# Moving the next sequence's norms into the MLP passes, and the last attention group's rotated rows ahead of weight loads

## The chip, the cores and the metric

The kernel runs on all 8 cores of one Trainium2 chip, as the same program on different data: each core computes two sequences of the batch of 16. The metric is the device time of the slowest core, in microseconds (us). Cores 0 to 3 are one die of the chip and cores 4 to 7 the other. In some executions of before the cores of one die show a lower granted clock of TensorE than the other die's and take longer: in one run of before 0.930 to 0.940 and 2206.7 to 2223.7 us on cores 4 to 7, against 0.973 to 0.977 and 2133.2 to 2148.7 us on cores 0 to 3. Such runs are called slow and are not compared with fast ones.

## The reference

One layer of an encoder, then a final norm. Only the order of the parts matters here. Sequences have 2048 positions of 1024 channels, the memory has 256 positions, the MLP is 4096 wide.

```python
def reference(x, mem, norm_mix, w_in, ..., norm_final):
    h = rms_norm(x, norm_mix[l])                       # "norm 1"
    x = x + hybrid_mixer(h, ...)     # projections; DFT branch; 3 attention groups with
                                     # rotary on the first 16 of 64 head dims; gates; merge
    h = rms_norm(x, norm_cross[l])
    mem_n = rms_norm(mem, norm_mem[l])                 # "memory norm"
    x = x + memory_cross_attention(h, mem_n, ...)
    h = rms_norm(x, norm_mlp[l])
    x = x + sq_relu_mlp(h, w_up[l], w_down[l])
    return rms_norm(x, norm_final)                     # "final norm"
```

## The kernel before

A helper records every operation with its reads and writes and then sets the semaphores; so every instruction has the helper's line (L148) in the profile, and all of SBUF is one tile called `arena`. A sequence is worked in four tiles (`tg`) of 512 positions. "A unit" below is eight matmuls into one PSUM bank (PSUM is the memory that TensorE's matmuls write to, `ps` in the views) and what evicts it. In the views PE is TensorE, PEld its weight loads, DVE VectorE, ACT ScalarE, POOL GpSimd and SP SyncE.

**The norm.** Squares are made by ScalarE, added up over eight channel chunks by GpSimd (`eng='pool'`), split into a high and a low bf16 half, summed over partitions by two matmuls with a matrix of ones, and turned into a reciprocal root by ScalarE. VectorE then scales.

```python
def norm_sq(k, src, n=512, ns=0, eng='pool', lag=False):
    ...
    def add(i):
        if i > 0:
            tt(eng, acc_, acc_, sq[i % 2][:, 0:n], ALU.add)
    act(sq[k % 2][:, 0:n] if k else acc_, src, AF.Square)
    ...
    add(k)
    if k == 7:
        act(hi, acc_, AF.Copy)
        tt('dve', lo, acc_, hi, ALU.subtract)

def norm_rstd(n=512, ns=0, r=None):
    ...
    mm(o, ones, hi[:, 0:n], True, False)
    mm(o, ones, lo[:, 0:n], False, True)
    act(r, o, AF.Ln, scale=1.0 / D, bias=eps)
    act(r, r, AF.Exp, scale=-0.5)

pend = []                       # generators with work put off
def popp(fc, first=3, steps=2): # after unit fc: take `steps` steps of it, from unit `first` on
    ...
```

**The last MLP pass and the sequence boundary.** The MLP goes in four passes over a quarter of its width each; `xT` is the residual and stays in SBUF. In the last pass (3) the kernel also makes the final norm, and norm 1 of the next sequence's tiles 0 to 2.

```python
def up(p_, tg, nxt=None):
    for fc in range(8):
        ...                                       # 8 matmuls
        act(r_, psf(b), AF.Relu)
        tt('dve', a2T[tg % 2][:, fc, :], r_, r_, ALU.mult)
        if nxt is not None:
            norm1_sq(b_ + 1, nxt, [fc], ns=1)     # next sequence's squares
        popp(fc, 3, 4 if p_ == 3 and not last_seq else 2)

def down(p_, tg, t0=0, n=512):
    for fc in range(8):
        ...                                       # 8 matmuls
        tt('dve', x_, o, x_, ALU.add)
        if p_ == 3:
            norm_sq(fc, x_, n, ...)               # final norm's squares
        popp(fc, 3, 4 if p_ == 3 and not last_seq else 2)
...
up(3, 0)
up(3, 1, nxt(0))
down(3, 0)
pend.append(fin_out(0))                           # final norm: 8 scales, store
if not last_seq:
    pend.append(fin_next(0))                      # next sequence's norm 1: 8 scales
...                                               # the same for the tiles that follow
```

The next sequence begins with its projections. Its tile 3 and its memory are still not normed at that point:

```python
for tg in range(NTG):
    for i in range(6):
        ...                                       # projection units
    if tg == 0:
        flush()
        load_dft()                                # loads mem and the DFT matrix
        norm1_sq(b_, 3, ns=1)
    elif tg == 1:
        norm1_fin(b_, 3, ns=1)
        mem_sq()
    elif tg == 2:
        mem_fin()
```

**The rotated rows.** Of each head only 16 of 64 rows are rotated. They are gathered by small DMAs, rotated by VectorE, and put back by eight DMAs of 64 KB (`rb`). The attention of the group can't start before. For group 2 two weight loads of 1 MB each (`bload(3)`, `bload(4)`) were issued at about the same time.

```python
def rotate(g):
    ...
    for c in range(2):
        pairs = ...
        OP('sp', 'dma_group', pairs, reads=[rot], writes=[q_[:, c, :], k_[:, c, :]], dma_key='rb%d' % c)

def proj_gen(g):
    ...
    for i in range(8):
        if 2 <= i < 6:
            next(rg, None)                        # rotate, put back
        if i == 5:
            if g == 1:
                load_rope(2)
            else:
                bload(4)
        v_unit(g, 2 * i, FB)
        yield

interleave(attn(0), proj_gen(1), ...)
interleave(attn(1), proj_gen(2), ...)
bload(3)
...
interleave(attn(2), gate_first(), lambda k: k % 2)
```

**The start.** ScalarE casts the small Fourier weights in `load_consts` (`cp('act', fmb, fm32)`), and both halves of tile 0 are normed before the first projection unit.

The softmax here doesn't subtract the row's maximum and nothing guards it: scores larger than these inputs give would overflow.

## Time and profile before

| | before |
|---|---|
| time, median of 6 runs | 2147.29 us (2146.23 to 2207.45) |
| profiled execution, slowest core (5) | 2147.3 us |
| TensorE busy | 1992.4 us (93%) |
| TensorE idle | 147.4 us |
| mean granted TensorE clock, core 5 | 0.974 |

The page's first lines, the TensorE rows of its 40 slices, and the first line of the chain of waits. In the slices each digit is tenths: of TensorE's busy time in the row PE, of the granted clock in the row PEclk. One slice is 53.7 us.

```profile
span 2147.3 us, 30868 instructions; the slowest of 8 cores (2133.0 to 2147.3 us)
...
PE 1992.4 (93%) x10282; PEld 975.2 (45%) x10282; DVE 989.5 (46%) x1553; ACT 771.6 (36%) x1310; POOL 420.8 (20%) x391
...
PE   3789879999999999999878996999999999999996
...
PEclk9899999999999999999999998999999999999998
...
PE 82%; DVE 6%; ACT 4%; issue 3%; DMA 2%; POOL 2%; SPq 0%; ACTq 0%; DVEq 0%; POOLq 0%
```

TensorE bounds the kernel: 82% of the chain of waits is TensorE itself. What is left to gain is where the slices are below 9: the start (slices 1 to 3), slices 5 and 6 (the last attention groups of the first sequence), slices 20 to 22 (the boundary between the sequences), slice 25 (the last attention group of the second), and the end.

The windows view compares a pure MLP stretch with the boundary (core 5; the columns are the stretch, its length, then busy time with the number of instructions for PE, PEld, DVE, ACT and POOL, then granted clock, DMA share and GB/s).

```profile
660.00:1036.00 376.00, 376.00 (x1744) 170.48 (x1742) 133.81 (x229) 80.99 (x138) 34.49 (x34) 1.00 0.21 42
1036.00:1149.00 113.00, 88.19 (x365) 36.79 (x363) 77.72 (x101) 46.05 (x82) 56.80 (x49) 0.90 0.50 153
```

The MLP stretch has no idle TensorE and full clock, 0.2156 us a matmul (376 over 1744). At that pace the 365 matmuls of the boundary are worth 79 us; it took 113, with 24.8 us idle and a clock of 0.90. What TensorE waited for there (the waits view of core 5, us in total, times, longest):

```profile
PE ps L148 <- ACT arena L148: 21.8, 5, 4.9
PE ps L148 <- DVE arena L148: 3.0, 7, 0.7
```

Five waits for ScalarE, at the matmuls of five norms. From the order of the program and the number of matmuls between them they are the final norms of tiles 1 and 2 in the last pass, then, among the next sequence's projections, the final norm of tile 3, norm 1 of tile 3 and the memory norm. The timeline of core 0 shows them one by one (start, us, what ran, and in brackets the idle time before it and what ended it):

```profile
1044.80 0.59 PE L148 MATMUL ps<-arena 128*128 128x512 bf16 x1 [4.97 <-ACT arena L148]
...
1081.89 0.59 PE L148 MATMUL ps<-arena 128*128 128x512 bf16 x1 [4.97 <-ACT arena L148]
...
1107.31 0.38 PE L148 MATMUL ps<-arena 128*128 128x512 bf16 x1 [4.34 <-ACT arena L148]
...
1124.51 0.44 PE L148 MATMUL ps<-arena 128*128 128x512 bf16 x1 [4.22 <-ACT arena L148]
...
1139.14 0.27 PE L148 MATMUL ps<-arena 128*128 128x256 bf16 x1 [1.75 <-ACT arena L148]
```

The first two gaps lie in the last MLP pass, the other three in the next sequence's projections. A gap can cost more than itself: in it or at its end the granted clock mostly falls to 0.5 for 3.4 or 6.8 us (10.2 us before attention 2 on core 5). On core 5 the gap that ends at 1050.4 us goes with half clock from 1048.4 to 1055.2 us. At half clock matmuls start every 0.43 us (1051.3 to 1055.1 us), then every 0.2156 again.

Why ScalarE is late is seen on VectorE. Scale instructions of 128x512 f32 take 0.74 us alone (0.68 us each in a row) and twice that beside GpSimd's adds. The timeline of VectorE, core 5:

```profile
1055.79 4.54 DVE L148 SCALAR_TENSOR_TENSOR arena<-arena 128x512 f32<-128x512 f32 x3 [0.50 <-ACT arena L148]
...
1060.59 2.73 DVE L148 SCALAR_TENSOR_TENSOR arena<-arena 128x512 f32<-128x512 f32 x4
```

Three took 1.51 us each while GpSimd was adding squares (1.28 us an add), and the next four 0.68 us each when it was not. The trace shows the doubling, not what the two engines contend for. VectorE's next work is then late, ScalarE's squares of it are late (on core 5 ScalarE waited 33.3 us for VectorE between 1036 and 1149 us), and TensorE waits for the norm. The last of the five waits has one more cause: the load of the memory took 8.5 us from issue to landing, and ScalarE waited 5.9 us for it.

The rows of group 2, in the DMA view of core 5 between 247 and 256 us (out and in, queue, count, KB each, median us from issue to landing), and TensorE's timeline there:

```profile
arena<-wb POOLq DMA_DIRECT2D x2, 1024.0 KB, 11.7
arena<-arena SPq DMA_DIRECT2D x8, 64.0 KB, 9.4
```

```profile
261.50 2.00 PE L148 MATMUL ps<-arena 64*128 64x128 bf16 x11 [9.02 <-DMA arena<-arena]
```

Eight rows of 64 KB take 9.4 us beside two loads of 1 MB, and TensorE waits 9.02 us for them. Those of group 1, with no weight load issued beside them (193 to 198 us), take 2.3 us. So the rows of group 2 are slowed although they are on another queue than the loads.

### The profile page before, as it was taken

How to read it: one execution, taken by the hardware profiler on the slowest of the kernel's cores; microseconds unless marked ns; L12 is line 12 of the kernel's file. 1: busy time of each engine (PE TensorE's matmuls, PEld its weight loads, DVE VectorE, ACT ScalarE, POOL GpSimd, SP SyncE). 2: the span in 40 equal slices, each digit the busy share in tenths (PEclk: the TensorE clock that was granted, in tenths of full speed). 3: DMA queues.
4: the chain of work that ended last, by engine and by line, in shares of the span. 5: the costliest groups of instructions: out<-in, count | busy, mean ns of one | idle time of the engine just before them, and what ended most of it. 6: DMA issues, size and time to landing. Idle time of an engine off the chain costs nothing.

```text
span 2147.3 us, 30868 instructions; the slowest of 8 cores (2133.0 to 2147.3 us)
## 1 busy us (share of the span) xinstructions
PE 1992.4 (93%) x10282; PEld 975.2 (45%) x10282; DVE 989.5 (46%) x1553; ACT 771.6 (36%) x1310; POOL 420.8 (20%) x391
## 2 busy tenths in 40 slices
PE   3789879999999999999878996999999999999996
PEld 2445534455444444444334553444544444444443
DVE  4555572355453323233776456434545533333345
ACT  4445452246442120214434554423554311111143
POOL 2200013352330000004451000334413100000033
PEclk9899999999999999999999998999999999999998
DMA  8532406067020303121354422424540022121213
GB/s 211 115 75 59 79 19 178 1 118 128 11 79 1 68 11 59 20 50 30 130 150 117 85 60 50 157 40 79 93 85 1 1 40 40 30 50 20 40 40 118
DMA packets 32076, 147.04 MB, mean 68 GB/s; under 512 B 4529, under 2 KB 10802, under 8 KB 21682
## 3 DMA queue, kind: packets, MB, share of 16 engines
q0 software_dynamic: 11808, 75.50, 19.8%
q1 hardware_dynamic: 19680, 69.22, 9.8%
q8 instruction: 87, 1.43, 0.3%
q14 instruction: 67, 0.55, 0.1%
q10 hardware_dynamic: 434, 0.35, 0.1%
HBM read 197.48 MB, written 16.78 MB: 100 GB/s over the span
## 4 chain that ended last, share of the span: by engine, by line
PE 82%; DVE 6%; ACT 4%; issue 3%; DMA 2%; POOL 2%; SPq 0%; ACTq 0%; DVEq 0%; POOLq 0%
PE ps L148 82%; DVE arena L148 6%; ACT arena L148 3%; POOL arena L148 2%; DMA arena<-arena 1%; DMA arena<-mem 1%; DMA arena<-fmix 0%; SPq L146 0%; ACT L148 0%; DVEq L142 0%; ACTq L142 0%; POOLq L142 0%; ACTq L148 0%; SPq L148 0%; SPq L142 0%
## 5 line engine op out<-in xcount | busy, mean ns | idle before, releaser
L148 PE MATMUL ps<-arena 128*128 128x512 bf16 (+4 forms) x10282 | 1992.4, 357 | 147.4 <-ACT arena L148 92.8
L148 PEld LDWEIGHTS ps<-arena 128*128 128x128 bf16 (+1 forms) x10282 | 975.2, 100 | 1164.4 <-issue 247.4
L148 ACT ACTIVATE arena<-ps 128x512 bf16<-128x512 f32 (+4 forms) x812 | 488.9, 624 | 1001.3 <-PE ps L148 851.1
L148 DVE TENSOR_TENSOR arena<-arena 128x512 bf16<-128x512 bf16 (+7 forms) x607 | 315.0, 539 | 647.4 <-ACT arena L148 632.3
L148 POOL TENSOR_TENSOR arena<-arena 128x512 f32<-128x512 f32 (+2 forms) x299 | 366.6, 1227 | 746.2 <-ACT arena L148 461.5
L148 DVE TENSOR_TENSOR arena<-ps,arena 128x512 f32<-128x512 f32 (+3 forms) x376 | 293.3, 791 | 251.5 <-PE ps L148 250.4
L148 ACT ACTIVATE arena<-arena 128x512 f32<-128x512 f32 (+5 forms) x452 | 260.6, 589 | 340.9 <-DVE arena L148 203.0
L148 DVE SCALAR_TENSOR_TENSOR arena<-arena 128x512 bf16<-128x512 f32 (+3 forms) x296 | 218.4, 786 | 56.1 <-ACT arena L148 55.6
L148 POOL DMA_DIRECT2D arena<-wb x62 | 33.6, 543 | 778.8 <-PE ps L148 715.6
L148 DVE SCALAR_TENSOR_TENSOR arena<-arena,ps 128x512 f32<-128x512 f32 x128 | 81.9, 683 | 151.4 <-PE ps L148 146.8
L148 DVE SCALAR_TENSOR_TENSOR arena<-ps,arena 128x512 f32<-128x512 f32 x64 | 43.5, 687 | 32.8 <-PE ps L148 32.8
L148 ACT ACTIVATE arena<-ps,arena 128x512 f32<-128x512 f32 (+1 forms) x37 | 23.6, 638 | 21.1 <-DVE arena L148 16.2
L148 POOL DMA_DIRECT2D arena<-wa x20 | 10.9, 554 | 102.7 <-PE ps L148 101.6
L148 POOL MEMSET arena<- 128x2048 bf16 x6 | 10.9, 1812 | 89.3 <-PE ps L148 89.3
L148 DVE COPY arena<-ps 128x1024 f32<-128x1024 f32 (+3 forms) x20 | 20.2, 1009 | 6.3 <-PE ps L148 6.3
L148 DVE CAST arena<-ps 128x512 bf16<-128x512 f32 (+1 forms) x36 | 20.0, 580 | 4.4 <-PE ps L148 3.5
L148 DVE STREAM_SHUFFLE arena<-arena 128x2048 bf16<-128x2048 bf16 x6 | 13.7, 2287 | 0.0
L148 ACT ACT_TABLE_LOAD x9 | 11.5, 1283 | 5.9 <-PE ps L148 4.6
L148 DVE LOAD_MASK_SELECT arena<-arena x6 | 0.1, 14 | 3.4 <-DMA arena<-arena 3.4
L148 DVE CAST arena<-arena 128x1 bf16<-128x1 f32 x8 | 1.2, 153 | 0.4
L148 DVE MEMSET arena<- 128x1 bf16 (+2 forms) x6 | 0.8, 130 | 1.2 <-PEq L211 1.1
L211 POOL MEMSET const-float32-0.0<- 128x1 f32 x1 | 0.1, 99 | 0.5 <-issue 0.5
(3 smaller groups left out, 0.3 us busy)
## 6 DMA issues: line engine op xcount, KB each, us to landing
arena<-wb POOLq DMA_DIRECT2D x62, 1024.0 KB, 9.2
arena<-x SPq DMA_DIRECT2D x8, 2048.0 KB, 12.6
out<-arena SPq DMA_DIRECT2D x28, 512.0 KB, 2.7
arena<-x SPq DMA_DIRECT2D x24, 512.0 KB, 8.7
arena<-wa POOLq DMA_DIRECT2D x20, 512.0 KB, 9.3
arena<-rope SPq DMA_DIRECT2D x6, 1024.0 KB, 9.2
arena<-arena SPq DMA_DIRECT2D x96, 64.0 KB, 4.2
arena<-x SPq DMA_DIRECT2D x16, 256.0 KB, 10.8
```

What stands on the lines that cost most here:

```text
L148: ins = getattr(eo, o['name'])(*o['args'], **o['kw'])
L211: nc = bass.Bass("TRN2", target_bir_lowering=False)
```

## The change

The intent is to take three things off TensorE's way. Core of the diff, with cuts marked:

1. **Boundary.** The next sequence's x is loaded twice: in pass 1 its squares are made, in pass 2 the memory norm, and in pass 3 only the scales are left (from a second load of x in half tiles). The next sequence's projections then have no norm of their own to make; what is left there is the final norm of tile 3 and the last scales. The final norm's matmuls are taken from the second unit after it is queued (`popp(fc, 1)`) instead of the fourth, in both sequences. In the first sequence `popp` also takes two steps of put-off work a unit instead of four.

```diff
-    def up(p_, tg, nxt=None):
+    def up(p_, tg, hook=None):
...
-            if nxt is not None:
-                norm1_sq(b_ + 1, nxt, [fc], ns=1)
-            popp(fc, 3, 4 if p_ == 3 and not last_seq else 2)
+            if hook is not None:
+                hook(fc)
+            popp(fc, 1 if p_ == 3 else 3)
...                                        (popp in down() likewise)
+    rs = [view(Y0 + i * 2048, 512, F32) for i in range(NTG)]   # kept reciprocal roots
+    def fin_st(tg):
+        norm_rstd(512, 1, rs[tg])
+        yield
+    def sq_st(tg, fc):
+        norm_sq(fc, xst[:, fc, :], ns=1)
...
+    def fin_next(tg, b_=b_):               # pass 3: scales alone, 256 wide
+        for i in (2 * tg, 2 * tg + 1):
+            for c in range(8):
+                stt(hT[...], xh[i % 3][:, c, :], gains[:, 0, c:c + 1], rs[tg][...], ALU.mult, ALU.mult)
+                yield
+            if i + 3 < 8:
+                load_xh(i + 3)
...
+    def hook(tg):
+        if last_seq or p_ == 0:
+            return None
+        if p_ == 1:
+            return lambda fc: sq_st(tg, fc)
+        return (lambda fc: norm_sq(fc, memst2[:, fc, :], 256)) if tg == 1 else None
...
     # next sequence's projections
-    if tg == 0:
-        flush()
-        load_dft()
-        norm1_sq(b_, 3, ns=1)
-    elif tg == 1:
-        norm1_fin(b_, 3, ns=1)
-        mem_sq()
-    elif tg == 2:
-        mem_fin()
+        popp(i, 0, 2 if tg else 0)
+    load_dft()
```

2. **Rows.** Weight loads 3 and 4 are issued later and wait for group 2's rows; the last load of the rotary table is issued earlier in the projections.

```diff
-            bload(4)                       # in proj_gen(2), unit 5
-    bload(3)                               # after attention 1
+    if (n, k) == (0, 1):                   # in gate_first, beside attention 2
+        bload(3, back.values())            # back: the DMAs that put the rows back
+        bload(4, back.values())
```

3. **Start.** VectorE casts the Fourier weights where they are used, and the second half of tile 0 is finished after two projection units.

```diff
-    cp('act', fmb, fm32)
+    cp('dve', fmb, fm32)                   # in make_wz, later
...
-    for h in range(2):
-        norm1_sq(0, 0, ns=h, t0=h * 256, n=256, eng=0)
-        norm1_fin(0, 0, h, h * 256, 256)
-        wk = aload(1 + h)
+    norm1_sq(0, 0, ns=0, t0=0, n=256, eng=0)
+    norm1_fin(0, 0, 0, 0, 256)
+    aload(1)
+    norm1_sq(0, 0, ns=1, t0=256, n=256, eng=0)
+    wk = aload(2)
...
-    (0, 0, 256, {3: [lambda: sq1(0)]}),
+    (0, 0, 256, {1: [lambda: norm1_fin(0, 0, 1, 256, 256)], 3: [lambda: sq1(0)]}),
```

More of the change, by code (lines that the diff above doesn't have):

```diff
@@ L398, in bslot, with bload @@
             return view(R0 + BSLOT[n] * 8192, 4096)
-        def bload(n):
-            wdma(bslot(n), dr['wb'][n])
+        def bload(n, after=()):
+            wdma(bslot(n), dr['wb'][n], after)
         ASLOT = [2, 3, 0, 1, 6, 7, 4, 5, 6, 7]
@@ L412, in build_program @@
         xin = [view(o, 4096, F32, pat="p (c t) -> p c t", c=8) for o in (M0 + 16384, Y0, X0 + 16 * KB, X0 + 32 * KB)]
-        def xb(b_, tg):
-            return tg if b_ == 0 else tg % 2
         def load_xin(b_, tg, t0=0, n=512, after=()):
             src = dr['x'][b_, tg].rearrange("p (c t) -> p c t", c=8)
-            i = xb(b_, tg)
+            i = tg
             return [dma('sp', xin[i][:, 2 * h:2 * h + 2, t0:t0 + n], src[:, 2 * h:2 * h + 2, t0:t0 + n],
@@ L424, in norm1_sq @@
             for k in ks:
-                norm_sq(k, xin[xb(b_, tg)][:, k, t0:t0 + n], n, ns, eng)
+                norm_sq(k, xin[tg][:, k, t0:t0 + n], n, ns, eng)
         def norm1_fin(b_, tg, ns=0, t0=0, n=512):
             norm_rstd(n, ns)
-            norm_apply(0, [xin[xb(b_, tg)][:, c, t0:t0 + n] for c in range(8)],
+            norm_apply(0, [xin[tg][:, c, t0:t0 + n] for c in range(8)],
                        [hT[:, c, tg * 512 + t0:tg * 512 + t0 + n] for c in range(8)], n)
@@ L516, in gather @@
                 OP('sp', 'dma_group', rows, reads=[qkv_views(g)[which]], writes=[rot], dma_key='rg%d' % which)
+            back = {}
             def rotate(g):
@@ L528, in rotate @@
                     q_, k_, _ = qkv_views(g)
-                    OP('sp', 'dma_group', pairs, reads=[rot], writes=[q_[:, c, :], k_[:, c, :]], dma_key='rb%d' % c)
+                    back[c] = OP('sp', 'dma_group', pairs, reads=[rot], writes=[q_[:, c, :], k_[:, c, :]], dma_key='rb%d' % c)
             def v_unit(g, n0, banks):
@@ L609, in load_dft @@
             def load_dft():
-                dma('sp', memst, dr['mem'][b_].rearrange("p (c m) -> p c m", c=8), 'mem')
+                if b_ == 0:
+                    dma('sp', memst, dr['mem'][b_].rearrange("p (c m) -> p c m", c=8), 'mem')
                 dma('sp', dftm, dr['dft'].rearrange("p (k n t) -> p k n t", k=4, n=4), 'dft')
@@ L802, in proj_gen @@
                     qk_unit(g, which, c, tg, FB, 'act')
+                    if n == 1 and g == 2:
+                        load_rope(2)
                     if n == 7:
@@ L816, in proj_gen @@
                         next(rg, None)
-                    if i == 5:
-                        if g == 1:
-                            load_rope(2)
-                        else:
-                            bload(4)
                     v_unit(g, 2 * i, FB)
@@ L1050, in down @@
                         norm_sq(fc, x_, n, 0 if n == 512 else t0 // 256)
-                    popp(fc, 3, 4 if p_ == 3 and not last_seq else 2)
+                    popp(fc, 1 if p_ == 3 else 3)
             rstd2 = view(Y0 + 8192, 512, F32)
@@ L1067, in fin_out, with load_st @@
                     yield
-            for p_ in range(3):
-                up(p_, 0)
+            xst = view(M0 + 16384, 4096, F32, pat="p (c t) -> p c t", c=8)
+            xh = [view(o, 2048, F32, pat="p (c t) -> p c t", c=8) for o in (M0 + 16384, M0 + 24576, Y0 + 8192)]
+            rs = [view(Y0 + i * 2048, 512, F32) for i in range(NTG)]
+            def load_st(tg):
+                for h in range(4):
+                    dma('sp', xst[:, 2 * h:2 * h + 2, :], dr['x'][b_ + 1, tg].rearrange("p (c t) -> p c t", c=8)[:, 2 * h:2 * h + 2, :], 'st%d' % h)
@@ new lines, in fin_st, with load_xh @@
+            def fin_st(tg):
[3 more added lines that the diff above has]
+                norm_sq(fc, xst[:, fc, :], ns=1)
+                if fc == 7 and tg + 1 < NTG:
+                    load_st(tg + 1)
+            def load_xh(i):
+                tg, t0 = i // 2, i % 2 * 256
+                for h in range(2):
+                    dma('sp', xh[i % 3][:, 4 * h:4 * h + 4, :],
+                        dr['x'][b_ + 1, tg].rearrange("p (c t) -> p c t", c=8)[:, 4 * h:4 * h + 4, t0:t0 + 256], 'xh%d%d' % (i % 3, h))
@@ new lines, in fin_next, with mem_next @@
+            def fin_next(tg, b_=b_):
+                for i in (2 * tg, 2 * tg + 1):
+                    t0 = i % 2 * 256
+                    for c in range(8):
+                        stt(hT[:, c, tg * 512 + t0:tg * 512 + t0 + 256], xh[i % 3][:, c, :], gains[:, 0, c:c + 1],
+                            rs[tg][:, t0:t0 + 256], ALU.mult, ALU.mult)
+                        yield
+                    if i + 3 < 8:
+                        load_xh(i + 3)
+            def mem_next():
+                norm_rstd(256)
+                yield
+                for c in range(8):
+                    stt(memn[:, c, :], memst2[:, c, :], gains[:, 2, c:c + 1], rstd[:, 0:256], ALU.mult, ALU.mult)
+                    yield
@@ new lines, in build_program @@
+            memst2 = view(Y0 + 8192, 2048, F32, pat="p (c m) -> p c m", c=8)
+            for p_ in range(3):
+                def hook(tg):
[4 more added lines that the diff above has]
+                    return (lambda fc: norm_sq(fc, memst2[:, fc, :], 256)) if tg == 1 else None
+                if p_ == 1 and not last_seq:
+                    load_st(0)
+                    dma('sp', memst2, dr['mem'][b_ + 1].rearrange("p (c m) -> p c m", c=8), 'mem')
+                up(p_, 0, hook(0))
@@ L1071, in build_program @@
                 for tg in range(NTG):
+                    if p_ == 1 and not last_seq:
+                        pend.append(fin_st(tg))
+                    if p_ == 2 and tg == 1 and not last_seq:
+                        pend.append(mem_next())
                     if tg + 1 < NTG:
-                        up(p_, tg + 1)
+                        up(p_, tg + 1, hook(tg + 1))
                     if tg == NTG - 2:
@@ L1080, in build_program @@
                     bload(23 + 4 * p_)
-            nx = None if last_seq else b_ + 1
-            def fin_next(tg, b_=b_):
-                norm_rstd(ns=1)
-                yield
-                for c in range(8):
-                    stt(hT[:, c, tg * 512:(tg + 1) * 512], xin[tg % 2][:, c, :], gains[:, 0, c:c + 1], rstd, ALU.mult, ALU.mult)
-                    yield
-                if tg < 2:
-                    load_xin(b_ + 1, tg + 2)
-            def nxt(tg):
-                return None if last_seq else tg
             if not last_seq:
-                load_xin(b_ + 1, 0)
-                load_xin(b_ + 1, 1)
+                for i in range(3):
+                    load_xh(i)
                 aload(0)
                 aload(1)
-            up(3, 0)
-            up(3, 1, nxt(0))
-            down(3, 0)
-            pend.append(fin_out(0))
-            if not last_seq:
-                pend.append(fin_next(0))
-            up(3, 2, nxt(1))
-            down(3, 1)
-            pend.append(fin_out(1))
-            if not last_seq:
-                pend.append(fin_next(1))
-            up(3, 3, nxt(2))
-            if not last_seq:
-                aload(2)
-                aload(3)
-            down(3, 2)
-            pend.append(fin_out(2))
-            if not last_seq:
-                pend.append(fin_next(2))
+            for tg in range(NTG):
+                up(3, tg)
+                if not last_seq:
+                    pend.append(fin_next(tg))
+                    if tg == 3:
+                        aload(2)
+                        aload(3)
+                if tg:
+                    down(3, tg - 1)
+                    pend.append(fin_out(tg - 1))
             if last_seq:
```

## The prediction

> **What bounds it now.** The page: TensorE is busy 1992 of 2147 us, and the chain of waits is 82% TensorE. By windows, the pure matmul stages (320-625, 650-1036, 1365-1670, 1683-2110 us) have no idle TensorE. Loss sits at four places: the start (45.9 us idle up to 105 us), each sequence's last attention group (gaps of 9.0 us at 252.5 and 7.9 us at 1296.7), the sequence boundary 1036-1149 us (24.4 us idle), and the tail. Each gap is also followed by 3.4-10 us of 0.5 granted clock. [...]
>
> **The boundary.** Its 363 matmuls are worth 78 us at the undisturbed stages' pace; it takes 113 us. In the last MLP pass GpSimd adds squares for two norms (1.27 us each, two sets of seven per 27.5 us) while VectorE's scale instructions, 0.7-0.75 us alone, take about 1.54 us beside it [...]. VectorE lags a whole down-pass, then norms' matmuls wait 3.4-5 us, five times, the last three inside the next sequence (tile 3's norms, memory's). The change moves squares to pass 1 (ACT has room: 0.6+0.63 of 1.72 us a unit), memory norm to pass 2, and leaves pass 3 only scales (64 of 0.41 us for 32 of 0.7) with half of GpSimd's adds. It loads x again (8.4 MB, DMA nearly idle). [...] Gain 32 us.
>
> **Rotated rows.** Alone they land in 2.28 us (attention group 1); in group 2, among two weight loads, in 7-10 us. With the loads behind them the last needed row lands about 1 us after TensorE runs out: saves 8.0 and 7.0 us of idle, plus 2 us each of half clock: 19 us.
>
> **Start.** ACT waits 11.1 us for the small Fourier weights; x itself is complete at 14.5 us, so this gives about 1.4 us. Units ahead of the second half's norm give 2 us. Gain 3.5 us.
>
> **Loss.** In the last pass the final norm's matmuls are now placed after two units instead of four. Their operands come 4.6 us after the down-pass ends, two units are 3.4 us: about 1.15 us twice, and 1 us at the tail. Cost 3.3 us.
>
> Sum: 2147 - 32 - 19 - 3.5 + 3.3 = 2096, plus 2 for what I miss.
>
> **Predicted: 2098 us, 2086 to 2113.** Chances: faster by over 2% 0.72, within 2% 0.27, slower 0.01.
>
> **Right if:** between the last MLP passes of sequence 0 and its successor's V projection TensorE is busy at full clock with under 4 us idle; MLP pass 1 shows GpSimd and ACT busier and TensorE still full; rows of group 2 land in about 2.3 us, the gaps before attention 2 shrink to 1 us, weight loads follow them.
>
> **Wrong if:** VectorE and GpSimd saturate in pass 3 (gaps of several us at the final norm persist); scales wait for the second x load and block VectorE; the Fourier matrix load collides with sequence 1's first rotated rows; attention 2 turns out bound by ACT and VectorE.

2147 - 32 - 19 - 3.5 + 3.3 is 2095.8, put as 2096, and 2098 with the 2 us for what I missed. A term of the boundary's 32 us is an estimate that 2 to 3 us of waits would remain in pass 3; without it the boundary is the 35 us between 113 and 78. Two phrases go further than the trace of before, core 5: not each gap is followed by half clock (those of 19.3 and 8.9 us at the very start are not), and the DMA engines that were to load x again were 0.21 busy between 660 and 1036 us.

## The result and the profile after

| | before | after |
|---|---|---|
| time, median (lowest to highest; runs) | 2146.46 us (2143.63 to 2207.45; 20) | 2097.47 us (2094.72 to 2099.19; 10) |
| ratio of fast runs, with 95% interval | 1 | 0.9765 (0.9748 to 0.9782) |
| TensorE idle, core 5 | 147.4 us | 101.8 us |
| mean clock, core 5 | 0.974 | 0.983 |
| read from HBM | 197.48 MB | 205.87 MB |

Ratios here and below are the mean time of one kernel's fast runs over the mean of the other's of the same rounds, so they are not quite the ratio of the medians quoted beside them.

```profile
span 2115.7 us, 30871 instructions; the slowest of 8 cores (2089.6 to 2115.7 us)
...
PE 2007.4 (95%) x10282; PEld 980.3 (46%) x10282; DVE 982.1 (46%) x1586; ACT 771.5 (36%) x1309; POOL 418.8 (20%) x391
...
PE   4889979999999999999999988999999999999996
...
PEclk9989999999999999999999999999999999999887
...
PE 84%; DVE 5%; ACT 4%; issue 3%; DMA 2%; POOL 2%; SPq 1%; ACTq 0%; DVEq 0%; POOLq 0%
```

The page is of core 2, at 2115.7 us, while the median is 2097. The cores view says why:

```profile
core 2: 2115.7 us, clock 0.970
...
core 5: 2089.6 us, clock 0.983
...
die 1 (median of its cores): 2092.6 us, clock 0.983
```

In this execution the cores of die 0 had long stretches at a clock of 0.81: cores 2 and 3 for 159 us from 1933.8 and 1933.6 us of their spans (the last slices of PEclk show it for core 2), cores 0 and 1 most of the time from 35 to 195 us of theirs. What set it off the traces do not show. The eleven other runs of the same kernel do not show it (clocks of 0.981 to 0.985 on every core), so everything below is read from die 1, most of it from core 5.

The stages that answer to those shown of before, core 5:

```profile
660.00:1012.00 352.00, 352.00 (x1634) 159.68 (x1633) 138.35 (x255) 95.43 (x170) 56.67 (x55) 1.00 0.34 78
1012.00:1093.00 81.00, 81.00 (x377) 36.71 (x376) 60.93 (x102) 28.80 (x48) 32.70 (x28) 1.00 0.51 135
```

The boundary now runs as the MLP does: no idle, full clock, 0.2149 us a matmul. In the waits view TensorE has no wait at all between 986 and 1110 us, where before it had twelve. In the earlier window GpSimd and ScalarE took on work (56.7 us against 34.5, and 95.4 against 81.0) and TensorE did not notice. In the last pass the scales are narrower and less stretched (0.57 us where 0.48 is the time with no add beside them; in before, core 0, the two full-width forms took 0.87 and 0.96 us where 0.74 is the time alone), and GpSimd has 28 adds where before it had 45 (core 0, 975 to 1090 us). The groups of VectorE and GpSimd by form, core 5, 960 to 1080 us (busy, mean ns of one, idle before):

```profile
L148 DVE SCALAR_TENSOR_TENSOR arena<-arena 128x256 bf16<-128x256 f32 x64 | 33.7, 566 | 0.0
...
L148 POOL TENSOR_TENSOR arena<-arena 128x512 f32<-128x512 f32 x28 | 36.9, 1318 | 70.7 <-ACT arena L148 70.6 <-POOL arena L148 0.2
```

The rows of group 2, in the same two views (DMA from 242 to 252 us):

```profile
arena<-wb POOLq DMA_DIRECT2D x2, 1024.0 KB, 10.7
arena<-arena SPq DMA_DIRECT2D x8, 64.0 KB, 2.3
```

```profile
247.62 5.19 PE L148 MATMUL ps<-arena 64*128 64x128 bf16 x48 [0.98 <-DMA arena<-arena]
```

They land in 2.3 us, and the wait is 0.98 us.

Where the time came from, as the mean over the four cores of die 1 in the two profiled executions. The stages are cut at places that both traces have:

| stage | before, us | after, us | gain |
|---|---|---|---|
| start to the last matmul before attention 2 | 251.6 | 248.1 | 3.6 |
| from there to the wait before the branch units (rows) | 49.7 | 42.4 | 7.4 |
| from there to the first norm of sequence 0's mixer | 333.2 | 334.3 | -1.1 |
| from there to attention 0 of sequence 1 (boundary) | 537.6 | 502.5 | 35.1 |
| to attention 2 of sequence 1 | 120.6 | 120.9 | -0.3 |
| rows, sequence 1 | 52.8 | 47.3 | 5.5 |
| the mixer of sequence 1 | 329.2 | 328.6 | 0.6 |
| the rest, with the last MLP pass and the tail | 465.5 | 468.6 | -3.1 |
| sum | 2140.2 | 2092.6 | 47.5 |

The entries are rounded one by one. The first line should not be trusted to a microsecond: the moment at which a core reaches attention 2 differs by up to 11 us between the cores of one execution.

### The profile page after: what moved, and what is told of

It reads as the page before. It is cut to its first block, busy times and chain, and to the rows that moved or that the text cites. A ratio compares the mean times of both kernels' runs of the same rounds, so it can differ in the third digit from the quotient of the medians.

```text
span 2115.7 us, 30871 instructions; the slowest of 8 cores (2089.6 to 2115.7 us)
## 1 busy us (share of the span) xinstructions
PE 2007.4 (95%) x10282; PEld 980.3 (46%) x10282; DVE 982.1 (46%) x1586; ACT 771.5 (36%) x1309; POOL 418.8 (20%) x391
## 3 DMA queue, kind: packets, MB, share of 16 engines
HBM read 205.87 MB, written 16.78 MB: 105 GB/s over the span
## 4 chain that ended last, share of the span: by engine, by line
PE 84%; DVE 5%; ACT 4%; issue 3%; DMA 2%; POOL 2%; SPq 1%; ACTq 0%; DVEq 0%; POOLq 0%
PE ps L148 84%; DVE arena L148 5%; ACT arena L148 4%; POOL arena L148 2%; DMA arena<-arena 1%; DMA arena<-x 1%; SPq L146 0%; DMA arena<-wa 0%; ACT L148 0%; ACTq L142 0%; DVEq L142 0%; SPq L148 0%; POOLq L142 0%; SPq L142 0%
## 5 line engine op out<-in xcount | busy, mean ns | idle before, releaser
L148 DVE TENSOR_TENSOR arena<-arena 128x512 bf16<-128x512 bf16 (+8 forms) x607 | 310.8, 531 | 610.3 <-ACT arena L148 595.0
L148 ACT ACTIVATE arena<-arena 128x512 f32<-128x512 f32 (+3 forms) x451 | 261.4, 590 | 330.4 <-DVE arena L148 200.8
```

What stands on the lines that cost most here:

```text
L148: ins = getattr(eo, o['name'])(*o['args'], **o['kw'])
```

## The experiments

Edits are against the kernel named. "Us" are medians.

### The three parts alone

**rows_only**: before, with part 2 of the diff and nothing else.

> The kernel before with the row part alone: the two weight loads wait for the rotated rows, and the last rotation table is loaded earlier. My theory (the rows are slow only because two weight loads are in flight with them): rows of the last group land in about 2.3 us, the TensorE gaps ahead of attention 2 shrink from 5-9 us (5 on even cores, 9 on odd) to about 1 us, total 16 us faster than before (2130, range 2126 to 2135). Rival (attention 2 is bound by ACT and VectorE, earlier rows only move the wait into it): the gap shrinks but the total moves by under 5 us.

Measured: 2132.66 us, ratio 0.9926 (0.9914 to 0.9938), 16 us less. The waits before attention 2 were 0.98 to 1.05 us on every core of the trace, where before they were 5 to 6 or 9. As expected.

**start_only**: before, with part 3 and nothing else.

> The kernel before with the start part alone: the cast of the small Fourier matrix moved off ACT's queue, and the second half tile's norm placed after two projection units. My theory: 3 to 5 us faster (2142), seen as an earlier first square on ACT and an earlier end of the first projections. Rival (the first 50 us are bound by the arrival of x, DMA engines 75-91% busy there): under 1.5 us.

Measured: 2146.54 us, ratio 0.9993 (0.9979 to 1.0006): 1.5 us less by the means, and the interval includes nothing at all. The change did what it said at the start. ScalarE's wait for the Fourier weights is gone from the timeline of core 5, first before, then in this run:

```profile
13.89 2.92 ACT L148 ACTIVATE arena<-arena 128x128 bf16<-128x128 f32 x9 [11.12 <-DMA arena<-fmix]
```

```profile
5.47 0.72 ACT L148 ACTIVATE arena<-arena 128x256 f32<-128x256 f32 x2 [2.69 <-DMA arena<-x]
```

TensorE reached the DFT stage at 113.9 us instead of 116.6, as the mean of eight cores. Then attention 0 waits for the rotated rows of group 0, which travel beside weight loads 0 and 1. Core 4, before and in this run:

```profile
135.86 7.50 PE L148 MATMUL ps<-arena 64*128 64x192 bf16 x30 [5.86 <-DMA arena<-arena]
```

```profile
135.13 1.62 PE L148 MATMUL ps<-arena 64*128 64x192 bf16 x6 [7.95 <-DMA arena<-arena]
```

TensorE arrived earlier and waited longer: as the mean of eight cores attention 0 began at 135.0 us instead of 136.5. At attention 2 the mean lead was 0.8 us. A miss, with the gain turned into a wait. It is not the rival's case either: had the arrival of x held the start up, there would be no lead at the DFT stage.

**boundary_only**: before, with part 1, but with the last sequence's final norm left where it was.

```diff
-    popp(fc, 1 if p_ == 3 else 3)
+    popp(fc, 1 if p_ == 3 and not last_seq else 3)
```

> The kernel before with the boundary part alone (next sequence's squares in MLP pass 1, memory norm in pass 2, scales from a second load of x in pass 3), with the last sequence's final norms left where they were. My theory: the five gaps of 3-5 us between 1036 and 1149 us and their half-clock stretches go, total 34 us faster (2112, range 2107 to 2117). Rival (new waits in pass 3, for VectorE or the second x load, give a good part back): gaps of several us stay in pass 3 and the gain is under 28 us.

Measured: three of six runs were slow, so the median (2171.47) says nothing. The fast ones took 2113.83, 2114.39 and 2117.05 us, ratio 0.9846 (0.9831 to 0.9861), 33 us less. As expected.

**tail_undone**: after, with the same one-line edit, so that only the last sequence's placement of the final norm goes back.

> The changed kernel with one thing undone: in the last sequence's last MLP pass the final norm's matmuls come after four units again, not two. My theory: the change lost 2 to 3 us there, so this is 2 to 3 us faster than the changed kernel (2094.5), with no gap at the first two final norms of that pass. Rival (the earlier placement only moves a wait that the tail has anyway): within 1 us of the changed kernel.

Measured: 2094.38 us, ratio 0.975 (0.9737 to 0.9763), 3.1 us faster than the median of after. The timelines of TensorE on core 5, after and this kernel:

```profile
1996.56 0.38 PE L148 MATMUL ps<-arena 128*128 128x512 bf16 x1 [0.56 <-ACT arena L148]
...
2025.88 0.38 PE L148 MATMUL ps<-arena 128*128 128x512 bf16 x1 [0.56 <-ACT arena L148]
...
2055.27 0.38 PE L148 MATMUL ps<-arena 128*128 128x512 bf16 x1 [2.26 <-ACT arena L148]
```

```profile
1984.67 67.76 PE L148 MATMUL ps<-arena 128*128 128x512 bf16 x329
2052.95 0.38 PE L148 MATMUL ps<-arena 128*128 128x512 bf16 x1 [0.53 <-ACT arena L148]
```

Three waits at the final norms become one short one. So this part of the change is a loss. As expected. (After and this kernel were timed in different rounds; their ratios to before, 0.9765 and 0.975, give the same 3 us.) The kernel ran once more beside later ones:

> The same kernel as tail_undone once more, on the chip of the next two, so that they can be compared with it: 2094.4, within 2 us.

Measured: 2094.48 us, ratio 0.9752. The same.

The parts add up: 16 + 1.5 + 33 - 3 is 47.5 us, and the medians of the whole differ by 49.

### What made the boundary slow: GpSimd's adds, or where the norms stood

Two theories. The first is contention: GpSimd's adds of two norms at once slow VectorE in the last pass. The second is placement: norms of tile 3 and of the memory stand inside the next sequence's projections and have a chain of their own that nothing hides. One experiment takes the adds away from before, the other puts adds into after.

**no_adds**: before, where GpSimd does not add the next sequence's squares in pass 3. The first chunk's square, times eight, stands for the sum. It was meant to give a wrong result; it still passed the comparison.

```diff
-    if i > 0:
+    if i > 0 and eng != 'none':
         tt(eng, acc_, acc_, sq[i % 2][:, 0:n], ALU.add)
-    act(sq[k % 2][:, 0:n] if k else acc_, src, AF.Square)
+    act(sq[k % 2][:, 0:n] if k else acc_, src, AF.Square, scale=2.8284 if eng == 'none' else 1.0)
...
-    norm1_sq(b_ + 1, nxt, [fc], ns=1)
+    norm1_sq(b_ + 1, nxt, [fc], ns=1, eng='none')
```

> Wrong result on purpose: the kernel before, but GpSimd does not add the next sequence's squares in the last MLP pass (ACT still makes them; the norm is taken from one chunk of eight, scaled). All matmuls, VectorE's scales, loads and the order stay. My theory (GpSimd's adds hold VectorE up, VectorE then lags a whole pass): the scales there fall from about 1.5 to about 0.75 us, the two gaps of 4.95 us inside the pass and their half-clock stretches go, 12 to 17 us faster than before (2131). Rival (the gaps are the latency of the norm chains, whose matmuls are placed too early): both gaps stay, under 4 us.

Measured: 2151.77 us over all eight runs. Three were slow, two more had some cores at a lower clock (2146.62 and 2156.92 us); the three clean ones took 2138.3 to 2139.2 us against 2145.0 to 2150.5 for the undisturbed runs of before on that chip. The ratio 0.9974 (0.9941 to 1.0006) is no difference, because some disturbed runs are counted in it. The trace gives the size: from the DFT stage of one sequence to that of the next took 1044 us instead of 1052, as the mean of eight cores, so about 8 us. A miss: I had expected 12 to 17. The gaps of core 0, to be read against the five of before:

```profile
1045.42 0.38 PE L148 MATMUL ps<-arena 128*128 128x512 bf16 x1 [1.36 <-ACT arena L148]
...
1078.05 0.38 PE L148 MATMUL ps<-arena 128*128 128x512 bf16 x1 [3.37 <-ACT arena L148]
...
1103.44 0.58 PE L148 MATMUL ps<-arena 128*128 128x512 bf16 x1 [5.02 <-ACT arena L148]
...
1120.63 0.59 PE L148 MATMUL ps<-arena 128*128 128x512 bf16 x1 [3.22 <-ACT arena L148]
...
1136.87 0.27 PE L148 MATMUL ps<-arena 128*128 128x256 bf16 x1 [2.36 <-ACT arena L148]
```

The two gaps in the pass shrank from 4.97 and 4.97 to 1.36 and 3.37 us (on cores 2, 4, 5 and 7 to 1.4 and 1.7 us, where the third gap grew to 6.5). The three gaps in the next sequence stayed. These adds were not their cause.

**ballast**: after, with 24 useless GpSimd adds in pass 3 of sequence 0, eight for each of three tiles, where the next norm had seven. The result stays right.

```diff
+    def ballast(tg):
+        if last_seq or tg == 0:
+            return None
+        r = rs[3] if tg < 3 else rs[0]
+        return lambda fc: tt('pool', sq[1], r, r, ALU.add)
...
-        up(3, tg)
+        up(3, tg, ballast(tg))
```

> The changed kernel with GpSimd's load put back where it was and nothing else: eight adds of 128x512 f32 in each of the up passes 1 to 3 of the last MLP pass of the first sequence, on data that nobody needs; the result stays right. My theory [...]: scales get slower there, gaps of several us at the final norms come back with half-clock stretches, 8 to 20 us slower than the changed kernel (2105 to 2118). Rival (what was won is the shorter chain of norms and loads in the next sequence's prologue, GpSimd's load doesn't matter): within 2 us of the changed kernel.

Measured: 2112.86 us (clean runs 2109.6 to 2112.9), ratio 0.9855 (0.9814 to 0.9896), 12 to 15 us slower than after by the clean runs; from DFT stage to DFT stage 1024.8 us instead of 1011.4. As expected. On core 0, where after has nothing of the kind:

```profile
1039.41 0.59 PE L148 MATMUL ps<-arena 128*128 128x512 bf16 x1 [5.17 <-ACT arena L148]
...
1073.39 0.38 PE L148 MATMUL ps<-arena 128*128 128x512 bf16 x1 [3.51 <-ACT arena L148]
1074.22 51.05 PE L148 MATMUL ps<-arena 128*128 128x512 bf16 x228 [0.45 <-DVE arena L148]
```

The two gaps of the pass are back, on all eight cores (5.2 and 2.8 to 3.5 us), and none of the three others. The same scales are slower, in the groups of VectorE between 960 and 1080 us on core 0 (566 ns in after, on core 0 too):

```profile
L148 DVE SCALAR_TENSOR_TENSOR arena<-arena 128x256 bf16<-128x256 f32 x64 | 45.5, 751 | 0.0
```

One rival to VectorE as the link is that the useless adds only stand in GpSimd's queue ahead of the final norm's own adds. They do not: in ballast GpSimd is idle right before the first of these, for 10.2 us ahead of the first gap and some 5 us ahead of the second, on every core.

What follows: the two gaps inside the pass are mostly the work of GpSimd's adds, which are worth 8 to 13 us with what follows the gaps; 1.4 and 1.7 to 3.4 us of them remain without the adds. The three gaps in the next sequence are not their work: they stay without the adds and do not come back with them. Two of them belong to norms that the change moved out of that place, which fits the second theory. The third belongs to the final norm of tile 3, which after the change stands almost where it stood and no longer waits. The timeline of VectorE in before, core 5, shows what it waited for:

```profile
1105.35 3.73 DVE L148 SCALAR_TENSOR_TENSOR arena<-arena 128x512 bf16<-128x512 f32 x4
...
1109.01 0.68 DVE L148 TENSOR_TENSOR arena<-ps,arena 128x512 f32<-128x512 f32 x1
```

The down pass's last add stands behind four scales that `popp` had queued in that unit, and its square, the last add on GpSimd and the norm's matmul (1112.90 us) come after it. The change queues two a unit; no run took this apart. The rest of the 33 us, 20 to 25, is put down to these three gaps and their half clock by subtraction alone.

### Order or wait: what made the rows fast

**order_no_wait**: after, where the two loads stand late but do not wait for the rows.

```diff
-    bload(3, back.values())
-    bload(4, back.values())
+    bload(3)
+    bload(4)
```

> The changed kernel, with the two weight loads at their new place in the order but without the wait for the rotated rows (the buffers' own dependencies stay). Theory A (what counts is that the loads come later in the order, behind the V projection's last read of their buffer; the rows that attention 2 needs first have nearly landed by then): within 2 us of the changed kernel, the first four rows still land within 3 us of their issue. Theory B (the explicit wait is what protects the rows): rows take 6 to 10 us again, 8 us or more slower.

Measured: the three clean runs of seven took 2094.95 to 2097.37 us, the same as after (the median, 2106.38, holds disturbed runs; ratio 0.9784, 0.9744 to 0.9825, verdict unclear). The median of the rows is that of after (DMA view of core 5, 245 to 262 us):

```profile
arena<-arena SPq DMA_DIRECT2D x8, 64.0 KB, 2.3
```

The median hides the last three of the eight, which took 5.2, 8.0 and 9.6 us on core 5 and 4 to 10 us on every core. The first five took 2.2 to 2.3 us, and the wait before attention 2 was 0.97 to 1.04 us on every core. So the later place in the program is what counts here: it brings the first rows in, and the explicit wait protects only the later ones, which cost no time.

### What the experiments pointed to

**group0**: the wait that ate the start's gain is the rows' wait of another group. The kernel is tail_undone, with weight loads 0 and 1 behind group 0's rows.

```diff
-    bload(0)
-    bload(1)
+    bload(0, back.values())
+    bload(1, back.values())
```

> The changed kernel with the last sequence's final norms put back (as tail_undone) and one more use of the row idea: the two weight loads that follow the first attention group's rotation wait for its rows too. In the first sequence those rows now take about 10 us beside these loads and TensorE waits 4 to 8 us ahead of attention 0. My theory (rows are slow only because of the loads in flight; this wait also ate the start part's gain): rows land in 2.3 us, the gap falls under 1 us, 6 to 9 us faster than tail_undone (2087). Rival (the rows are late because VectorE's folds and rotation end late): the gap shrinks by under 3 us and the total moves by under 3 us.

Measured: 2087.61 us, ratio 0.9716 (0.9692 to 0.974), 7 us faster than tail_undone. As expected, but for the wait, which fell to 2.04 us on every core (ended by ScalarE) and not under 1 us. Attention 0 on core 5, in after and in this kernel:

```profile
132.83 10.34 PE L148 MATMUL ps<-arena 64*128 64x192 bf16 x50 [7.23 <-DMA arena<-arena]
```

```profile
129.63 13.55 PE L148 MATMUL ps<-arena 64*128 64x192 bf16 x67 [2.04 <-ACT arena L148]
```

The rows took 9.4 us in after and 2.3 here. At attention 2 the mean of eight cores is 243.1 us instead of 250.5 in tail_undone. This fits why start_only gave so little: TensorE waited at this place in it.

**fill**: one gap of about 8 us was left in each kernel, ahead of the branch units, with a half clock in and after it (after, core 5: a gap of 8.11 us to 297.4 us, a clock of 0.5 from 292.9 to 303.1). The kernel is tail_undone, with useless matmuls meant to keep the clock up.

```diff
     branch(n)
+    if n == 0:
+        b = ALLB[(P.rr[ALLB] - 1) % 8]
+        for _ in range(28 if b_ == 0 else 8):
+            mm(psf(b), wbr[:, 0, 0, 0:128], yfT[:, 0, 0:512], True, True)
```

> tail_undone with matmuls that nobody needs (28 of 512 columns in the first sequence, 8 in the second) put into the gap of 8 us (2.5 to 4 us) that TensorE has between attention 2 and the branch projections, into a bank that is free then; nothing waits for less. My theory (a gap costs its half-clock stretch as well): no stretch of 0.5 clock follows that gap, 2 to 4 us faster than tail_undone_2. Rival (what follows is bound by ACT's tanh and VectorE, so the clock does not matter there): the stretch goes, the total stays within 1 us.

Measured: 2104.93 us, ratio 0.9812 (0.9789 to 0.9836), 10 us slower. A miss, and by my own mistake. I had called the bank free. It is the one that branch 0's last result is read from, so the matmuls waited for that read and ran after the gap instead of in it (timeline of core 5):

```profile
301.94 4.42 PE L148 MATMUL ps<-arena 128*128 128x512 bf16 x10 [9.04 <-DVE arena L148]
```

**best**: group0 with the same edit.

> group0 with the filling matmuls of fill: if the parts add, 7 us faster than fill and 9 to 11 us faster than tail_undone_2 (2084).

Measured: 2097.1 us, ratio 0.9762, 9.5 us slower than group0, for the same reason. A miss.

**group0_fill**: the useless matmuls placed ahead of branch 0, in the bank that comes next and is free there.

```diff
+    if n == 0:
+        b = ALLB[P.rr[ALLB] % 8]
+        for _ in range(34 if b_ == 0 else 10):
+            mm(psf(b), wbr[:, 0, 0, 0:128], yfT[:, 0, 0:512], True, True)
     branch(n)
```

> group0 with the filling matmuls where a bank is free: 34 (second sequence 10) of 512 columns between the gates and the first branch projection, so that they end before the wait of 8 us (2.6 to 4 us) does. In fill they stood after that projection, whose bank is held until the wait's end, so they came after the gap and cost 7 to 10 us. My theory: the gap shrinks to about 1 us, the 10 us stretch of half clock behind it goes, 2 to 4 us faster than group0 (2084.5). Rival: what follows is bound by ACT and VectorE, or the stretch only moves: within 1 us of group0 (2087.6).

Measured: 2085.89 us (2082.66 to 2086.66), ratio 0.9701 (0.9688 to 0.9714). The gap is filled and the clock stays up. Windows of core 5, group0 and then this kernel:

```profile
285.00:302.00 17.00, 8.87 (x28) 3.19 (x27) 12.67 (x20) 11.50 (x19) 4.56 (x4) 0.70 0.00 0
```

```profile
285.00:302.00 17.00, 16.23 (x75) 6.91 (x74) 13.71 (x22) 11.38 (x19) 6.09 (x5) 1.00 0.00 0
```

It is the fastest kernel measured and beats before by 3%. Against group0 the gain is some 2 us, with overlapping intervals (the stage from attention 2 to the next sequence took 873.0 us against 875.0). The useless matmuls save only the half clock, not the gap itself: on core 5 the next useful matmul comes at 294.91 us, in group0 at 295.04.

## Why the prediction was right, and where it was not

I predicted 2098 us and the median was 2097.47.

- **Boundary, "Gain 32 us".** Right: 33 alone. The mechanism was only half as I told it. I put contention first and the norms in the next sequence as its follow-up; no_adds and ballast show that the adds are worth only 8 to 13 us, and that the three gaps in the next sequence have another cause. My estimate that 2 to 3 us of waits would remain failed: no wait remains. The scales took 0.57 us on average (counted over the trace of core 5 of after: 0.48 with no add at the same time, 0.67 with one), where I had counted with 0.41 (at the start of before such scales follow each other every 0.40 us); where my estimate was too high was not worked out.
- **Rows, "19 us".** Right in mechanism, a little large: 16 alone. The rows land in 2.3 us and the wait is 1 us, as I said. On core 5 the idle terms came out as predicted, 9.02 to 0.98 us and 7.94 to 0.95. The mis-sized term is "plus 2 us each of half clock": the two stages became 8.4 and 7.7 us shorter, so it was 0.4 and 0.7. Part of the half clock only moved: after the change 3.4 us of it come at the next gap (2.87 us, to 255.7 us), where before there was none. Core 5 was also among the slower cores; others waited only about 5 us before, which is why the mean of die 1 shows 7.4 and 5.5.
- **Start, "Gain 3.5 us".** This is the step that failed. The early lead of 2.7 us was there, and attention 0 spent it waiting for group 0's rows, which no part of the change touched. Measured alone: 1.5 us, not to be told from nothing. group0, which frees those rows, is worth 7 us.
- **Loss, "Cost 3.3 us".** Right: 3.1. tail_undone takes it back. I had 1.15 us twice and 1 us at the tail; the trace shows 0.56 us twice and 2.26 once, each followed by 0.4 us, so the sum fits better than its parts.
- **"plus 2 for what I miss".** The start gave 2 us less and the rows 3 less, the boundary 1 more. The margin took up half of that; the rest is as small as the scatter of the medians. So it is partly luck that the total fits to within 1 us.
- **What would have made it wrong** did not occur. Scales did not wait for the second load of x, which landed in 4.0 us, and the DFT matrix did not hold up the first rows of sequence 1.

Some things stay open. The metric gained 49 us, and the mean core of die 1 gained 47.5: in before one core of each neighbouring pair was about 10 us behind the other (2133.0 and 2144.1, 2134.6 and 2144.2, 2134.3 and 2147.3, 2134.3 and 2144.7 us in the profiled execution). The rows part takes most of that away. Over the fast, undisturbed runs the mean difference within a pair is 10.0 to 10.4 us in before, 10.4 in start_only, 9.9 in boundary_only and 10.6 in no_adds, but 5.2 in rows_only and 3 to 4 in every kernel that holds the rows part with others. The trace of before agrees: ahead of attention 2 one core of a pair waits 9 us for the rows and the other 5 to 6, in the second sequence 7 to 8 and 5. Why the rows come later to one core of a pair was not tested.

## What to carry to other kernels

When a stage shows waits for a norm, separate the two causes before moving anything: other work that slows the engines beside it (here scales of 0.68 us took 1.51 us beside GpSimd's adds), and a chain that stands where nothing hides it. Small transfers that start the next stage belong ahead of the large loads in program order (here eight rows of 64 KB took 9.4 us beside two loads of 1 MB and 2.3 us ahead of them); look for the same pattern at every place where it occurs, for a gain ahead of an unmended one is only waited away (here a lead of 2.7 us at the DFT stage was 1.5 us at attention 0). If matmuls are put into a gap to keep the clock (group0_fill: 1.00 instead of 0.70), check that their PSUM bank is not waiting for the very thing that the gap waits for (fill: they began after a gap of 9.04 us).
